# Block 2's mixers: gates by ScalarE's own Silu, a 31-tap convolution over 1024 tokens with its sums in SBUF, and mixer C queued behind it

## The chip, the cores and the metric

The kernel runs on one core of one Trainium2 chip. Its engines work side by side, each on its own list of instructions in a fixed order: PE (TensorE, the matmuls), DVE (VectorE), ACT (ScalarE), POOL (GpSimd) and SP (SyncE, which here issues most of the DMAs). Semaphores tie the lists together: an instruction waits until those it reads from have ended, and all that stands behind it on its engine waits with it. The metric is the device time of one launch in microseconds (us), lower is better. Accumulators of matmuls lie in PSUM, everything else that the engines compute on in SBUF.

## The reference

Two transformer-like blocks over 1024 tokens of width 1024; the change touches only the second, `mix` of the reference. Its input `h` (normalised and modulated) is projected into eleven slots of 512 channels, which feed four mixers; what they give is gated, joined and projected back:

```python
def mix(h, lp, h0, pool_fn):
    proj = jnp.einsum('btd,de->bte', h, lp['w_in'])
    (va, za, bb, bc, bv, zb, ca, cg, zc, dv, zd) = jnp.split(proj, N_IN_SLOTS, axis=-1)
    ya, h_final = rglru(va, lp, h0)
    yb = bb * depthwise_conv(bc * bv, lp['b_conv'], B_CONV // 2, B_CONV // 2)
    u = ca * jax.nn.sigmoid(cg)
    u = depthwise_conv(u, lp['c_conv'], C_CONV // 2, C_CONV // 2)     # C_CONV = 31 taps
    u = layer_norm(u, lp['c_ln_g'], lp['c_ln_b'])
    yc = jnp.einsum('btc,ce->bte', jax.nn.silu(u), lp['c_pw']) + lp['c_pw_b']
    p = pool_fn(dv)
    ...
    cat = jnp.concatenate([ya * jax.nn.silu(za), yb * jax.nn.silu(zb),
                           yc * jax.nn.silu(zc), yd * jax.nn.silu(zd)], axis=-1)
    return jnp.einsum('bte,ed->btd', cat, lp['w_out']), h_final
```

Here silu(z) = z * sigmoid(z), and the depthwise convolution with 31 taps adds, for each channel, 31 shifted copies of its 1024 tokens, each times its own weight.

## The kernel before

Channels lie on the 128 partitions, tokens along the free axis, and the 1024 tokens are two halves of 512 (`HS`). Every large product is made of three matmuls of 128x128 by 128x512: both operands are split into a high part (rounded to fp32r by ACT, a CAST, "hi") and the rest (by DVE, "lo"), and hi·hi, hi·lo and lo·hi are added up in PSUM (lines 411 to 413). A 128x1024 block of weights comes by DMA on SP's queue into a raw tile `wr` and is split into `wh` (ACT, line 367) and `wl` (DVE, line 368); there are three of each, so a raw tile is loaded again only when the `wl` that reads it is done.

`mixers_in` (line 2030 on) computes Block 2's projections with `p2`, one 128-channel chunk of a slot at a time, 8 products a half, on PE from the high/low tiles `kk` of the input. Gates and values that are needed later go to DRAM through `keep` (tile `pk`). The mixers are generators that yield a cost after each step and stand in lists; `tick(n, q)` runs steps of a list until their costs reach n. `fill(a, b)` between two projections runs 4 units (`FA`) of the background list `bg` (mixers A and D) and 3 units (`FB`) of the list `convs`. So the order in which the program is written down mixes projections with mixer steps.

- Mixer A (`mixer_a`, `rg_gates`, `rg_decay`, `rg_scan`; tiles `va`, `xc`, `xh`) is a gated recurrence, mixer D (`mixer_d`; `ph`, `pl`) a box mean followed by a small product.
- Mixer B is written in line at the end of `mixers_in` (`m`, `y`, and the gate `sg` at lines 2092 to 2094).
- Mixer C: `c_in` makes `u` = 2·ca·sigmoid(cg) (tiles `cu`). `conv31` (line 2011) adds the 31 taps of one 128-channel chunk up in two PSUM tiles `pp`, one for a half, so each tap is two instructions of DVE; ACT copies the sums back into `cu` (2028). When all four are done, at c = 3 of the last loop, the rest of `convs` is run to its end (2074) and `mixer_c` is put in `bg` (2076). `mixer_c`, for one half after the other: adds the four chunks (`la`), means by a matmul with ones (`mu`), squares (`acc`, ones matmul at 465), `rs` by Ln and Exp (447, 448), then for each chunk `ln`, `lt` and `sc` (2127 to 2134), and for each output chunk its weights `wch`/`wcl`, 12 matmuls, `yc` (2144) and the product with its gate (`cz`, `cat_out`).

A silu is made of the Tanh function on ACT and DVE instructions, with factors 0.5 folded in: z·sigmoid(z) = 0.5·(tanh(z/2)+1)·z. ACT holds one set of function tables at a time; where the next function lies in another set, an ACT_TABLE_LOAD stands before it.

`tail` projects the joined outputs back: `dense(pair, half, ticks)` loads eight tiles `cr` of `cat` from DRAM, splits them into `cx` (ACT 469, DVE 470), and runs 8 output chunks of 24 matmuls, with 5 units of `bg` after each in the first two calls. What is left of `bg` is flushed before `dense(1, 0)`.

The instructions are not issued in written order. The kernel records them and a list scheduler inside it sets the order on each engine by estimated costs and by data and tile dependences; that order is fixed when the program is built.

Of the kernel before, what the change touches and what calls it, by code (L numbers as in the profile page):

```python
# [11 lines left out]
AF = mybir.ActivationFunctionType  # L12
ALU = mybir.AluOpType
# [5 lines left out]
T = 1024  # L19
HALF = 512  # L20
# [278 lines left out]
HS = [slice(0, HALF), slice(HALF, T)]  # L299


class Build:
# [1680 lines left out]
    def keep(self, slot, c, silu=False):  # L1983

        nc = self.nc
        d = self.dp.tile([P, T], F32, name=f"p2{slot}{c}")

        def epi(ps, sl, hf):
            t = self.F2("pk")
            if silu:  # L1990
                nc.scalar.activation(t, ps, AF.Tanh, scale=0.5)
                nc.vector.scalar_tensor_tensor(t, t, 1.0, ps, op0=ALU.add, op1=ALU.mult)
            else:
                nc.scalar.copy(t, ps)
            self.dma(d[:, sl], t, q="scalar")
        self.p2(slot, c, epi)
        return d

    def cat_out(self, i, c, y, z, hf):

        t = self.T2("cz")
        self.dma(t, z[:, HS[hf]])
        self.nc.vector.scalar_tensor_tensor(t, y, 0.5, t, op0=ALU.mult, op1=ALU.mult)
        self.cat_store(i, c, t, hf)

    def cat_store(self, i, c, t, hf):
# [1 line left out]
        self.dma(d, t, q="scalar")  # L2008
        self.cat[i, c, hf] = d

    def conv31(self, c, u):

        nc = self.nc
        w = lambda j: self.CW[:, 31 * c + j:31 * c + j + 1]
        acc = [self.pp(), self.pp()]
        for hf, sl in enumerate(HS):
            nc.vector.tensor_scalar(acc[hf], u[:, sl], w(15), None, op0=ALU.mult)
        for j in range(31):
            s = j - 15
            if s == 0:  # L2020
                continue
            for hf in range(2):
                a, b = max(HALF * hf, -s), min(HALF * hf + HALF, T - s)
                o = acc[hf][:, a - HALF * hf:b - HALF * hf]
                nc.vector.scalar_tensor_tensor(o, u[:, a + s:b + s], w(j), o, op0=ALU.mult, op1=ALU.add)  # L2025
            yield 1.3
        for hf, sl in enumerate(HS):
            nc.scalar.copy(u[:, sl], acc[hf])

    def mixers_in(self):  # L2030

        self.wide = False
        nc = self.nc
        self.za, self.zd, self.zc = {}, {}, {}
        o = VOFF["c_conv"]
        self.CW = self.V[:, o:o + 124]
        nc.gpsimd.tensor_scalar(self.CW, self.V[:, o:o + 124], 0.5, None, op0=ALU.mult)
        cus = [None] * 4
        m, y = self.S("bm"), self.S("by")
        convs = []  # L2040

        def fill(a, b):
            self.tick(a)
            self.tick(b, convs)

        def c_in(c, halves, ticks):
            if cus[c] is None:
                cus[c] = self.S("cu")
            u = cus[c]
            self.p2(7, c, lambda ps, sl, hf: nc.scalar.activation(u[:, sl], ps, AF.Tanh, scale=0.5), ticks, halves)  # L2050
            self.p2(6, c, lambda ps, sl, hf: nc.vector.scalar_tensor_tensor(u[:, sl], u[:, sl], 1.0, ps, op0=ALU.add, op1=ALU.mult),
                    ticks, halves)
        for c in range(4):
            c_in(c, (0,), N3)
        self.flush()
        for c in range(4):
            c_in(c, (1,), 0)
            convs.append(self.conv31(c, cus[c]))
            fill(0, 6)
        for c in (3, 2, 1, 0):  # L2060
            v, u = self.keep(0, c), self.keep(9, c)
            self.behind(self.mixer_a(c, v))
            self.behind(self.mixer_d(c, u))
            fill(FA, FB)
            fill(FA, FB)
            self.za[c] = self.keep(1, c, True)
            fill(FA, FB)
            self.zd[c] = self.keep(10, c, True)
            fill(FA, FB)
        for c in range(4):  # L2070
            self.zc[c] = self.keep(8, c, True)
            fill(FA, FB)
        for c in range(4):
            if c == 3:
                while convs:
                    self.tick(1, convs)
                self.behind(self.mixer_c(cus))
            self.p2(3, c, lambda ps, sl, hf: nc.scalar.copy(m[:, sl], ps))
            fill(FA, FB)
            self.p2(4, c, lambda ps, sl, hf: nc.vector.tensor_mul(m[:, sl], m[:, sl], ps))  # L2080
            w = lambda tap: self.vec("b_conv", 3 * c + tap)
            nc.scalar.mul(y, m, w(1))
            nc.vector.scalar_tensor_tensor(y[:, 1:], m[:, :T - 1], w(0), y[:, 1:], op0=ALU.mult, op1=ALU.add)
            nc.vector.scalar_tensor_tensor(y[:, :T - 1], m[:, 1:], w(2), y[:, :T - 1], op0=ALU.mult, op1=ALU.add)
            fill(FA, FB)
            self.p2(2, c, lambda ps, sl, hf: nc.vector.tensor_mul(y[:, sl], y[:, sl], ps))
            self.dump(f"y_b{c}", y)
            fill(FA, FB)

            def epi(ps, sl, hf):  # L2090
                t = self.F2("sg")
                nc.scalar.activation(t, ps, AF.Tanh, scale=0.5)
                nc.vector.scalar_tensor_tensor(t, t, 1.0, ps, op0=ALU.add, op1=ALU.mult)
                nc.vector.scalar_tensor_tensor(t, y[:, sl], 0.5, t, op0=ALU.mult, op1=ALU.mult)
                self.cat_store(1, c, t, hf)
            self.p2(5, c, epi)
            fill(FA, FB)

    def mixer_c(self, us):

# [215 lines left out]
```

## Time and profile before

| | us |
|---|---|
| median of 3 runs | 2543.75 (2543.48 to 2548.24) |
| profiled execution | 2544.9 |
| its span, first to last instruction | 2543.1 |
| PE busy | 2476.3 (97%) |
| DVE, ACT busy | 1727.1 (68%), 1188.1 (47%) |
| Block 2's mixers and tail, by the timeline | about 1810 to 2330, and 2330 to 2543 |

Times in rows of the profile are in us from the start of the span unless marked ns. `mm<-cx,wh` reads "a matmul that writes the PSUM tile mm from cx and wh"; `[1.34 <-ACT cx L469]` says that the engine stood idle for 1.34 us before this instruction and that the write of `cx` by ACT at line 469 ended the wait. Matmuls overlap: each is shown longer than the distance between their starts. ACT's instructions overlap a little too.

### The profile page before, as it was taken

What the parts mean: (1) busy time and instruction counts of PE and PEld (TensorE: products, weight loads), DVE (VectorE), ACT (ScalarE), POOL (GpSimd) and SP (SyncE); (2) the same over time, 40 slices, a digit from 0 to 9 for tenths busy, and PEclk for the clock granted to TensorE, in tenths of its full rate; (3) what the DMA queues carried; (4) which work ended last, traced back from release to release, by engine and by line L of the source; (5) the groups of instructions that cost most, each with busy time, mean ns of one, the idle gap of its engine ahead of it and who ended that gap; (6) DMA issues with size and microseconds to landing.
All of it is one profiled execution on the core that took longest, in us unless ns stands there. A gap on an engine that the chain in (4) does not pass through costs nothing. (4 is left out here: it accounts for less than half of the span.)

```text
span 2543.1 us, 33781 instructions
## 1 busy us (share of the span) xinstructions
PE 2476.3 (97%) x12732; PEld 2004.7 (79%) x12732; DVE 1727.1 (68%) x2647; ACT 1188.1 (47%) x1843; POOL 182.1 (7%) x238
## 2 busy tenths in 40 slices
PE   8999999999999999999999999999999999999997
PEld 7887888776777678877788888887888888887886
DVE  7536765664755436758867864457798999996744
ACT  5425554622514357147644543435536355445623
POOL 0000000120111111630000000000000000000000
PEclk9999999999999799999999999999999999999998
DMA  6365443683775567868676565556533333325732
GB/s 218 106 210 160 140 134 105 186 250 104 230 205 157 164 210 233 287 193 278 235 257 221 180 204 180 187 187 224 183 119 113 133 134 97 113 91 192 247 100 100
DMA packets 180085, 449.23 MB, mean 177 GB/s; under 512 B 32145, under 2 KB 42257, under 8 KB 179921
## 3 DMA queue, kind: packets, MB, share of 16 engines
q1 hardware_dynamic: 141504, 342.44, 40.5%
q0 software_dynamic: 18576, 64.63, 9.1%
q10 hardware_dynamic: 19840, 40.00, 4.3%
q8 instruction: 100, 1.64, 0.3%
q14 instruction: 65, 0.52, 0.1%
HBM read 321.55 MB, written 125.44 MB: 176 GB/s over the span
## 5 line engine op out<-in xcount | busy, mean ns | idle before, releaser
L367 ACT CAST wh<-wr 128x1024 fp32r<-128x1024 f32 x243 | 255.0, 1049 | 496.3 <-PE mm L412 246.5
L368 DVE TENSOR_TENSOR wl<-wr,wh 128x1024 fp32r<-128x1024 f32 x243 | 299.5, 1233 | 222.4 <-ACT wh L367 215.9
L411 PE MATMUL mm<-h,wh 128*128 128x512 f32 x760 | 308.1, 406 | 4.0 <-ACT h L469 2.1
L412 PE MATMUL mm<-h,wh 128*128 128x512 f32 x760 | 305.9, 403 | 0.8 <-DVE h L470 0.8
L413 PE MATMUL mm<-h,wl 128*128 128x512 f32 x760 | 304.7, 401 | 0.0
L411 PE MATMUL mm<-kk,wh 128*128 128x512 f32 x704 | 275.2, 391 | 0.0
L412 PE MATMUL mm<-kk,wh 128*128 128x512 f32 x704 | 274.5, 390 | 0.5 <-DVE kk L1811 0.5
L413 PE MATMUL mm<-kk,wl 128*128 128x512 f32 x704 | 274.0, 389 | 0.0
L411 PEld LDWEIGHTS mm<-h,wh 128*128 128x128 f32 x760 | 144.9, 191 | 37.2 <-ACT h L469 3.3
L412 PEld LDWEIGHTS mm<-h,wh 128*128 128x128 f32 x760 | 144.9, 191 | 33.7 <-issue 3.6
L413 PEld LDWEIGHTS mm<-h,wl 128*128 128x128 f32 x760 | 144.6, 190 | 32.7 <-issue 2.9
L2025 DVE SCALAR_TENSOR_TENSOR pp<-cu,vec,pp 128x512 f32<-128x512 f32 (+9 forms) x240 | 166.3, 746 | 0.1
L412 PEld LDWEIGHTS mm<-kk,wh 128*128 128x128 f32 x704 | 132.1, 188 | 29.1 <-issue 1.0
L411 PEld LDWEIGHTS mm<-kk,wh 128*128 128x128 f32 x704 | 132.1, 188 | 28.3 <-issue 0.7
L413 PEld LDWEIGHTS mm<-kk,wl 128*128 128x128 f32 x704 | 132.1, 188 | 27.7 <-issue 0.2
L1539 PE MATMUL pp<-h,wh 128*128 128x512 f32 x320 | 126.2, 397 | 3.8 <-ACT x L1606 2.2
L1540 PE MATMUL pp<-h,wh 128*128 128x512 f32 x320 | 124.8, 390 | 1.4 <-DVE h L470 1.4
L1541 PE MATMUL pp<-h,wl 128*128 128x512 f32 x320 | 123.6, 389 | 0.0
L1748 PE MATMUL pp<-bl,wh 128*128 128x512 f32 x304 | 120.1, 395 | 2.4 <-DVE bl L470 1.7
L1749 PE MATMUL pp<-bh,wl 128*128 128x512 f32 x304 | 119.1, 392 | 0.0
L1747 PE MATMUL pp<-bh,wh 128*128 128x512 f32 x304 | 116.5, 391 | 1.6 <-ACT bh L474 1.6
L411 PE MATMUL mm<-cx,wh 128*128 128x512 f32 x256 | 99.8, 391 | 1.3 <-ACT cx L469 1.3
(562 smaller groups left out, 5434.8 us busy)
## 6 DMA issues: line engine op xcount, KB each, us to landing
wr<-in_wi_dram SPq DMA_DIRECT2D x77, 512.0 KB, 3.4
ws<-in_wm_dram POOLq DMA_DIRECT2D x48, 512.0 KB, 5.8
wr<-in_wo_dram SPq DMA_DIRECT2D x48, 512.0 KB, 3.7
wr<-in_wg_dram SPq DMA_DIRECT2D x32, 512.0 KB, 4.4
gt<-gt POOLq DMA_DIRECT2D x64, 256.0 KB, 4.6
g<-gt SPq DMA_DIRECT2D x64, 256.0 KB, 4.9
wm<-in_wm_dram SPq DMA_DIRECT2D x32, 512.0 KB, 5.0
br<-buB SPq DMA_DIRECT2D x32, 512.0 KB
```

Source lines behind the costliest of these rows:

```text
L367: self.nc.scalar.copy(hi, raw)
L368: self.nc.vector.tensor_sub(lo, raw, hi.bitcast(F32))
L411: M(ps, lhsT=ah, rhs=bh, start=start and i == 0, stop=False)
L412: M(ps, lhsT=ah, rhs=bl, start=False, stop=False)
L413: M(ps, lhsT=al, rhs=bh, start=False, stop=stop and i == last)
L1539: M(ps, lhsT=ah, rhs=bh, start=start and i == 0, stop=False, skip_group_check=True)
L1540: M(ps, lhsT=ah, rhs=bl, start=False, stop=False, skip_group_check=True)
L1541: M(ps, lhsT=al, rhs=bh, start=False, stop=i == last, skip_group_check=True)
L1747: M(banks[p], lhsT=wh[:, o], rhs=bh[:, r], start=first, stop=False, skip_group_check=True)
L1748: M(banks[p], lhsT=wh[:, o], rhs=bl[:, r], start=False, stop=False, skip_group_check=True)
L1749: M(banks[p], lhsT=wl[:, o], rhs=bh[:, r], start=False, stop=jj == 7 and e == 1, skip_group_check=True)
L2025: nc.vector.scalar_tensor_tensor(o, u[:, a + s:b + s], w(j), o, op0=ALU.mult, op1=ALU.add)
```

## The change

Three things are edited. Every silu of a gate from a projection (`keep` with `silu`, mixer B's `sg`) becomes one ACT instruction with the function Silu, and the multiplication with the gate becomes a plain `tensor_mul` on DVE; the silu inside `mixer_c` stays with Tanh. `conv31` works over all 1024 tokens in one SBUF tile `co` of the pool S, one DVE instruction a tap, whose first tap (j = 15) is an ACT multiplication; the copy back goes, and a tap yields 1.2 in place of 1.3. `mixer_c` is appended to `convs`, behind the last convolution, when the list is built; the run of `convs` to its end at c = 3 goes, and what is left of `convs` after the last projection is added to `bg`.

```diff
         def epi(ps, sl, hf):
             t = self.F2("pk")
             if silu:
-                nc.scalar.activation(t, ps, AF.Tanh, scale=0.5)
-                nc.vector.scalar_tensor_tensor(t, t, 1.0, ps, op0=ALU.add, op1=ALU.mult)
+                nc.scalar.activation(t, ps, AF.Silu)
...
-        self.nc.vector.scalar_tensor_tensor(t, y, 0.5, t, op0=ALU.mult, op1=ALU.mult)
+        self.nc.vector.tensor_mul(t, y, t)
         self.cat_store(i, c, t, hf)
...
-    def conv31(self, c, u):
+    def conv31(self, c, us):
         nc = self.nc
+        u = us[c]
         w = lambda j: self.CW[:, 31 * c + j:31 * c + j + 1]
-        acc = [self.pp(), self.pp()]
-        for hf, sl in enumerate(HS):
-            nc.vector.tensor_scalar(acc[hf], u[:, sl], w(15), None, op0=ALU.mult)
+        o = self.S("co")
+        nc.scalar.mul(o, u, w(15))
         for j in range(31):
             s = j - 15
             if s == 0:
                 continue
-            for hf in range(2):
-                a, b = max(HALF * hf, -s), min(HALF * hf + HALF, T - s)
-                o = acc[hf][:, a - HALF * hf:b - HALF * hf]
-                nc.vector.scalar_tensor_tensor(o, u[:, a + s:b + s], w(j), o, op0=ALU.mult, op1=ALU.add)
-            yield 1.3
-        for hf, sl in enumerate(HS):
-            nc.scalar.copy(u[:, sl], acc[hf])
+            a, b = max(0, -s), min(T, T - s)
+            nc.vector.scalar_tensor_tensor(o[:, a:b], u[:, a + s:b + s], w(j), o[:, a:b], op0=ALU.mult, op1=ALU.add)
+            yield 1.2
+        us[c] = o
...
             c_in(c, (1,), 0)
-            convs.append(self.conv31(c, cus[c]))
+            convs.append(self.conv31(c, cus))
+            if c == 3:
+                convs.append(self.mixer_c(cus))
             fill(0, 6)
...
         for c in range(4):
-            if c == 3:
-                while convs:
-                    self.tick(1, convs)
-                self.behind(self.mixer_c(cus))
             self.p2(3, c, lambda ps, sl, hf: nc.scalar.copy(m[:, sl], ps))
...
                 t = self.F2("sg")
-                nc.scalar.activation(t, ps, AF.Tanh, scale=0.5)
-                nc.vector.scalar_tensor_tensor(t, t, 1.0, ps, op0=ALU.add, op1=ALU.mult)
-                nc.vector.scalar_tensor_tensor(t, y[:, sl], 0.5, t, op0=ALU.mult, op1=ALU.mult)
+                nc.scalar.activation(t, ps, AF.Silu)
+                nc.vector.tensor_mul(t, y[:, sl], t)
                 self.cat_store(1, c, t, hf)
             self.p2(5, c, epi)
             fill(FA, FB)
+        self.bg += convs
```

The diff does not show what the scheduler makes of it. Each list below is one engine's order, first to last; a name carries the tile's number, and `<-` stands between what is written and what is read.

ACT, before, around the end of the projections: `sg_3665` is the last gate of mixer B (its PSUM tile is filled by the last projection), `yc_3670` an output of mixer C's first half, and `cx_3692` the first tile that the tail's matmuls read.

```order
L367 CAST wch_3667_19974<-wcr_3666_19973 128x512
L367 CAST wh_3724_20173<-wr_3723_20171 128x1024
L2092 ACTIVATE sg_3665_19967<-mm_3664_19942 128x512
L2144 ACTIVATE yc_3670_19992<-pp_3669_19979,vec_90 128x512
L469 CAST cx_3692_20065<-cr_3691_20063 128x512
L325 DMA cat131_19971<-sg_3665_19967 128x512
L469 CAST cx_3694_20070<-cr_3693_20068 128x512
```

ACT now, at the same place; `sg_3647` is that last gate, `lt` and `ln` belong to the layer norm of mixer C's first half, and `cx_3653` is the tail's first tile.

```order
L2123 ACTIVATE lt_3679_19853<-ln_3678_19851,sm_3622_19589 128x512
L2086 ACTIVATE sg_3647_19742<-mm_3646_19717 128x512
L2124 ACTIVATE ln_3678_19851<-ln_3678_19851,vec_90 128x512
L367 CAST wh_3693_19913<-wr_3692_19911 128x1024
L325 DMA cat131_19745<-sg_3647_19742 128x512
L469 CAST cx_3653_19765<-cr_3652_19763 128x512
L367 CAST wch_3681_19860<-wcr_3680_19859 128x512
L469 CAST cx_3655_19770<-cr_3654_19768 128x512
```

The layer norm of mixer C's first half stood far ahead of the tail's first tile, with some of that half's outputs between; now its last steps stand right before that tile, behind the last gate, and the outputs come later. On PE the ones matmul of that half's squares stood 121 rows ahead of the tail's first matmul (rows 10044 and 10165) and now stands 49 rows ahead of it (10092 and 10141); each of those 49 rows but the first is a projection on `kk`.

PE, before, in the second half of mixer C inside the tail, rows 10331 to 10336: `pp_3740` is the first product that reads the normalised `sc`, `mm_3772` a chunk of the tail's first half.

```order
L413 MATMUL mm_3772_20433<-cx_3704_20095,wl_3767_20398 128x512
L411 MATMUL mm_3772_20433<-cx_3706_20100,wh_3766_20397 128x512
L411 MATMUL pp_3740_20265<-sc_3684_20051,wch_3738_20260 128x512
L412 MATMUL pp_3740_20265<-sc_3684_20051,wch_3738_20260 128x512
L412 MATMUL mm_3772_20433<-cx_3706_20100,wh_3766_20397 128x512
L413 MATMUL mm_3772_20433<-cx_3706_20100,wl_3767_20398 128x512
```

PE now, the same place, rows 10382 to 10387: `pp_3740` is again that product, and `cx_3778` is the first tile of the tail's second half, `dense(0, 1)`.

```order
L413 MATMUL mm_3776_20329<-cx_3667_19800,wl_3771_20294 128x512
L411 MATMUL pp_3740_20129<-sc_3708_19995,wch_3738_20124 128x512
L412 MATMUL pp_3740_20129<-sc_3708_19995,wch_3738_20124 128x512
L411 MATMUL mm_3800_20409<-cx_3778_20357,wh_3774_20325 128x512
L411 MATMUL mm_3804_20441<-cx_3778_20357,wh_3798_20405 128x512
L413 MATMUL pp_3740_20129<-sc_3708_19995,wcl_3739_20125 128x512
```

The ones matmul of this half's squares stood at row 10270 and stands at 10341, so that from it to the first product on `sc` there were 63 rows and are 42. The first matmul on a tile of `dense(0, 1)` stood at row 10407, 137 rows behind the ones matmul, and stands at 10385, 44 behind it. PE's list up to row 8146 is the same in both programs, and each has 11010 rows; DVE's list goes from 2606 to 2445 rows, ACT's from 1895 to 1900. Of ACT_TABLE_LOADs from this stage on there were 28, and there are 37.

## Rows read from the trace of the kernel before

**Rows 1.** Page, busy time of each engine, its share of the span, x instructions.

```profile
PE 2476.3 (97%) x12732; PEld 2004.7 (79%) x12732; DVE 1727.1 (68%) x2647; ACT 1188.1 (47%) x1843; POOL 182.1 (7%) x238
```

**Rows 2.** Windows: sum, PE, PEld, DVE, ACT, POOL busy (records), clock, DMA share, GB/s.

```profile
1950.00:1975.00 25.00, 25.00 (x112) 20.71 (x111) 24.92 (x29) 14.96 (x20) 2.55 (x3) 1.00 0.27 95
...
2325.00:2350.00 25.00, 23.66 (x104) 19.14 (x103) 16.04 (x24) 10.73 (x18) 0.00 (x0) 1.00 0.83 297
```

**Rows 3.** Waits, waiter <- releaser: sum, count, longest; PE from 1800, SP 2200 to 2420.

```profile
PE pp L1394 <- DVE acc L1389: 2.3, 1, 2.3
...
PE pp L411 <- ACT ph L469: 1.5, 2, 1.1
...
PE mm L411 <- ACT cx L469: 1.3, 1, 1.3
...
SPq L372 <- DVE wl L368: 151.6, 23, 16.5
```

**Rows 4.** DVE groups, 1800 to the end: busy us, mean ns | idle before, releaser.

```profile
L2025 DVE SCALAR_TENSOR_TENSOR pp<-cu,vec,pp 128x512 f32<-128x512 f32 x120 | 89.4, 750 | 0.0
...
L2017 DVE TENSOR_SCALAR pp<-cu,vec 128x512 f32<-128x512 f32 x8 | 5.7, 747 | 0.0
...
L1850 DVE SCALAR_TENSOR_TENSOR xc<-va,vec,xc 128x1023 f32<-128x1023 f32 x4 | 5.1, 1285 | 5.2 <-ACT xc L1845 5.2
...
L1992 DVE SCALAR_TENSOR_TENSOR pk<-pk,mm 128x512 f32<-128x512 f32 x24 | 16.4, 684 | 0.6 <-ACT pk L1991 0.4
...
L2093 DVE SCALAR_TENSOR_TENSOR sg<-sg,mm 128x512 f32<-128x512 f32 x8 | 5.4, 681 | 4.8 <-ACT sg L2092 4.8
...
L470 DVE TENSOR_TENSOR cx<-cr,cx 128x512 fp32r<-128x512 f32 x32 | 20.6, 686 | 5.5 <-ACT cx L469 5.5
...
L368 DVE TENSOR_TENSOR wl<-wr,wh 128x1024 fp32r<-128x1024 f32 x84 | 102.6, 1221 | 17.6 <-ACT wh L367 16.0
```

**Rows 5.** ACT groups, same stretch and columns.

```profile
L2028 ACT COPY cu<-pp 128x512 f32<-128x512 f32 x8 | 4.6, 587 | 3.8 <-DVE pp L2025 3.3 <-ACT pk L1994 0.4
...
L1845 ACT ACTIVATE xc<-va,vec 128x1024 f32<-128x1024 f32 x8 | 9.2, 1151 | 2.8 <-DMA va<-p 2.8
...
L1991 ACT ACT_TABLE_LOAD x3 | 3.8, 1283 | 0.5 <-ACT pk L1994 0.4
```

**Rows 6.** Timeline of ACT, end of Block 2's mixers: start, length, [idle before <- releaser].

```profile
2312.86 0.71 ACT L2129 ACTIVATE lt<-ln,sm 128x512 f32<-128x512 f32 x1
...
2313.47 0.62 ACT L2133 ACTIVATE sc<-ln 128x512 fp32r<-128x512 f32 x1
...
2313.99 0.71 ACT L2130 ACTIVATE ln<-ln,vec 128x512 f32<-128x512 f32 x1
...
2329.01 1.05 ACT L367 CAST wh<-wr 128x1024 fp32r<-128x1024 f32 x1 [1.54 <-PE mm L412]
...
2329.97 0.59 ACT L2092 ACTIVATE sg<-mm 128x512 f32<-128x512 f32 x1
...
2332.61 0.61 ACT L469 CAST cx<-cr 128x512 fp32r<-128x512 f32 x1
```

**Rows 7.** Timeline of PE, the first matmul of the tail.

```profile
2333.27 0.97 PE L411 MATMUL mm<-cx,wh 128*128 128x512 f32 x3 [1.34 <-ACT cx L469]
```

**Rows 8.** Timeline of PE and ACT, second half of mixer C, inside the tail.

```profile
2357.92 1.03 PE L465 MATMUL pp<-acc,ones 128*128 128x512 f32 x2
...
2359.69 1.28 ACT L448 ACT_TABLE_LOAD   x1
...
2360.99 0.63 ACT L448 ACTIVATE rs<-rs 128x512 f32<-128x512 f32 x1
...
2371.40 0.62 ACT L367 CAST wch<-wcr 128x512 fp32r<-128x512 f32 x1 [0.25 <-DMA wcr<-in_wcp_dram]
...
2372.88 0.39 PE L411 MATMUL pp<-sc,wch 128*128 128x512 f32 x1
```

**Rows 9.** Tile cat: from a transfer's issue to its landing.

```profile
DMA to landing us min/median/max: 2.0/5.1/8.1
```

## The prediction

> **What bounds the kernel now.** The page's busy times come first: PE is busy for 97% of the span, DVE for 68%, ACT for 47% [rows 1]. So time can only come from what PE waits for, and the next view is the windows over Block 2's mixers and the tail. In the mixers DVE is as full as PE: from 1950 to 1975 it works for 24.92 of 25.00 us, ACT for 14.96, and PE for all 25.00 [rows 2]. Its window holds 112 records, about two of them cut at an edge, so PE starts a matmul every 25.00/110 = 0.227 us. From 2325 on PE has a hole (23.66 of 25.00) while DVE has fallen to 16.04. The third view, PE's waits from 1800 to the end, says how much a full DVE costs: nearly nothing. The largest are 2.3 us for the last `acc` at the very end, 1.5 us in two waits for mixer D's `ph`, and 1.3 us for `cx`, the tail's first tile [rows 3]; what is left adds up to about 1 us. An engine that is full beside a PE that does not wait is off the path. The last view is the order of instructions on ACT, DVE and PE at the two places where mixer C meets the tail, with lengths from the timelines [rows 6 to 8].
>
> **The change part by part.**
>
> Convolution. Before: 240 instructions of DVE on PSUM; the 120 full ones take 750 ns each, and the 120 that are a little narrower no more, so up to 179 us; with the 8 first taps (5.7 us) 185 us [rows 4]. Now: 120 on SBUF over 1009 to 1023 tokens. The trace has that shape in mixer A at 1285 ns, so 120 x 1.285 = 154 us at most, and DVE saves about 31 us. On ACT 8 copies go (4.6 us) and 4 multiplications of 1.15 us come (4.6 us): nothing. If a tap in SBUF cost as much as two halves (1.50 us), nothing is saved, and since PE does not wait for DVE there, nothing is lost either.
>
> Silu. On DVE 24 instructions of `keep` go (16.4 us) and 8 of mixer B (5.4 us) [rows 4]; the remaining products change form, not number. DVE in all: about -53 us, of which PE can collect only its own waits. I let the wait for `ph` go, which DVE's queue feeds: -1.3 of 1.5 us (bounds 0 and -1.5). Of the hole at the end nothing goes, since the last `acc` is far behind the change.
>
> Tables. Silu lies in another set than Sigmoid, and the program has 9 more ACT_TABLE_LOADs from this stage on. One takes 1283 ns [rows 5], so ACT gets 9 x 1.28 = 11.5 us more. In the mixers ACT works 14.96 of 25 us, and a projection's half gives it 24 x 0.227 = 5.4 us before the next result, so I take 0 there (bounds 0 and +11.5); if that cover is gone, each load delays the copy that frees a PSUM tile. In rows 8 the ACTIVATE behind a load starts 0.02 us after its end (2359.69 + 1.28, then 2360.99), so the load is the whole price seen. The Trainium skill, page "ScalarE: Activation LUTs", section "What ACT_TABLE_LOAD costs", puts a switch of sets at about 2.66 us, the load and a drain of about 1.38 us, and the section "Table sets: the hidden batching unit" has kernels group work by set. By the page the nine would take 24 us of ACT and my forecast would be 1.4 us higher, for the one load at the first place below; this trace shows the load's length and not the drain.
>
> First place: the tail's first matmul. `mixer_c` now runs behind the list of convolutions and not when the last convolution is forced, and so comes later against PE. From the ones matmul of its first half's squares to the tail's first matmul there were 121 rows of PE; there are 49. I set that ones matmul's start to 0 and replay the three lists. PE needs 0.63 us more for it than for others (rows 8: 14.96 us to the 63rd row behind it, 63 x 0.227 = 14.3), so PE arrives at 0.63 + 49 x 0.227 = 11.75. On ACT `rs` ends at 3.70 (2360.99 + 0.63 - 2357.92, with the same load in it), DVE gives the first `ln` at 4.5, and then ACT's list holds: `lt`, a load for Silu (1.28), `sg`, and `ln`, `lt` and `sc` of the chunks, at starts 0.61, 0.52 and 0.62 us apart [rows 6], with DVE's products in between (about 0.7 each), until the last `lt` ends at 12.25. Then come the last gate `sg_3647`, which needs PE's last projection, `ln_3678`, `wh_3693` (0.96 from start to start, rows 6) and `cx_3653` (0.61): `cx` is ready at about 15.05, a wait of 3.3. Its low part is on DVE behind `wl_3694` (1.22 us) and takes 0.69 [rows 4]: PE's second matmul waits 1.1 more, its fifth, behind `wcl`, about 0.65. And on SP the load of `wr_3749` stands ahead of the last three `cr`; it waits for `wl_3694` to free a raw tile, as SP did for 151.6 us in 23 waits of that kind [rows 3]. These `cr` then land 2.0 to 8.1 us after issue, 5.1 in the middle [rows 9]: PE gets there at about 20.2, the tiles at 18.6 to 24, so I add 1.0 (0 to 4). In all 3.3 + 1.75 + 1.0 = 6.05, less the 1.34 that PE waited there before [rows 7]: **+4.7**. Lower bound: only what stands on ACT behind PE's last projection, sg 0.5 + ln 0.62 + wh 0.96 + cx 0.61 = 2.7, so +1.4. Upper: no overlap on ACT (cx a further 0.95 later) and a late `cr`, +8.
>
> Second place: the second half of mixer C. From its ones matmul to the first product on `sc` there were 63 rows; there are 42. PE arrives at 0.63 + 42 x 0.227 = 10.2. Before, the weights `wch` were cast by 2372.02, 14.1 after the ones matmul, and PE came at 14.96 without a wait [rows 8]. Now a `wh` of 1 us less stands in that chain, and by the same replay `wch` ends at about 12.9: a wait of 2.7. Two rows later PE needs `cx_3778` of the tail's second half, which ACT casts behind `sc_3711`: 0.9 more; two rows later `wcl`, behind a `wl` and a `sc` on DVE: 0.8 more. **+4.4** (bounds +2, when the chain gains 0.7 and DVE is ahead, and +7.4, without overlap and with late `cr`). Before, `dense(0, 1)` began 137 rows behind the ones matmul and none of this was near.
>
> The sum: 4.7 + 4.4 - 1.3 = +7.8 on the profiled execution's 2544.9, that is 2552.7. That execution was 1.15 above the median of the runs shown, so the forecast on their scale is **2551.5 us**. About 0.2%, 5.1 us, is what a measurement of this kernel can tell from no change: slower begins at 2548.8, faster at 2538.7.
>
> **The rivals.**
>
> A, the forecast: both places make PE wait, about 2551.5. For it: the order on each engine is fixed, the chains behind the ones matmuls hold only work that the trace has lengths for, and PE brings too few rows to cover them. Against it: the order in which cr and weights arrive is not fixed.
>
> B, not slower: DVE's relief pays for the places. They cost their lower bounds, +1.4 and +2, because a DVE without a backlog answers ACT at once; and the waits before them go (`ph` 1.5 and about 1 for the others): 2543.75 + 3.4 - 2.5, about 2544.7. It decides if the two places together wait under 8 us (the 1.34 of before included), with DVE idle before each step of `ln`. For it: DVE falls by 53 us just ahead of the first place. Against it: these chains are mostly ACT's own instructions.
>
> C, the table loads reach PE as well. In the mixers a load before a `keep` or `sg` delays a PSUM tile that PE wants; half of the 11.5 us on top of the 7.8: 2543.75 + 7.8 + 5.8, about 2557, and 1.3 more if the wait for `ph` stays too. For it: loads stand right before copies that free PSUM tiles. Against it: of the 28 loads before none shows as a releaser in PE's waits, which name tiles that were late by 1.5 us in sum at most.
>
> D, faster: DVE was the hidden bound. Waits of 3.9 us vanish, and the tail's tiles are ready in time because all of mixer C runs earlier: 2544.9 - 3.9 - 1.15, about 2540. Against it: the order on PE itself puts mixer C's steps nearer to the tail, so C cannot run earlier than PE's own list allows.
>
> **How the numbers follow.** A 0.56, B 0.25, C 0.13, D 0.06. Slower by over 0.2% is A less a small part near its lower end, and C: 0.67. Within 0.2%: B and that part, 0.27. Faster: 0.06. The range goes from 2544.5, just under B (both lower bounds, and every other wait gone), which leaves out D and the part of B below it, to 2558, near both upper bounds (2543.75 + 15.4 - 1.3 = 2557.9) and the middle of C. A alone would be 2547 to 2557.
>
> **What would show it.** In the profile after: DVE's convolution as 120 instructions of about 1.28 us, and windows between 1950 and 2275 with DVE well below 25 us while PE stays at 25.00; no `ph` wait. PE's waits should hold 3 to 4 us for ACT's `cx` at the tail's first matmul, with `cx` of DVE or `cr` just behind, and some 4 us for `wch`, `cx` and `wcl` 42 to 46 rows after the second ones matmul. Right before the first, ACT's timeline should show the last gate, `ln`, `wh` and `cx` without a gap. The prediction is wrong if PE passes both places with under 3 us of wait (B or D), or if its waits before 2325 grow (C).

## The result and the profile after

The changed kernel is slower: 2566.03 us median of 6 launches (2553.77 to 2570.57) against 2543.61 for the kernel before on the same chip, a ratio of 1.0077 (95% interval 1.0048 to 1.0106). Measured again in 12 launches it was 1.0059 (1.0031 to 1.0086). The sign of the forecast was right, its size was not: +7.8 us were forecast, some 15 to 22 came, and 2566 lies above the range.

Launches of one program spread over 20 us here, so what moves by a few us is read from the traces. One stretch serves as a measure: from the first projection matmul of Block 2 (the first that reads `kk`) to the end. It starts at 1811.72 in the trace before and at 1803.69 in the trace after; what differs ahead of it is no work of the change (in the window from 840 to 860 the granted clock was 0.51 in the first and 0.83 in the second). The stretch took 2543.1 - 1811.72 = 731.4 us before and 2552.0 - 1803.69 = 748.3 after: +16.9. Second traces of the two kernels gave 730.5 and 749.6.

The page after, line of busy times, against [rows 1]: DVE fell by 39 us (53 were forecast) and ACT rose by 13, PE's own work is the same.

```profile
PE 2476.8 (97%) x12732; PEld 2004.9 (79%) x12732; DVE 1687.8 (66%) x2487; ACT 1201.0 (47%) x1848; POOL 182.1 (7%) x238
```

The window that [rows 2] shows, after the change: DVE was to be well below 25 us there and is not. It has room in other windows (11.71 of 25 us from 1925 on, 16.50 from 2125 on).

```profile
1950.00:1975.00 25.00, 25.00 (x112) 20.70 (x111) 25.00 (x26) 8.09 (x13) 2.55 (x3) 1.00 0.32 116
```

PE's waits from 1800 to the end of the trace after, the view of [rows 3]:

```profile
PE mm L411 <- ACT cx L469: 4.5, 2, 4.1
PE pp L411 <- ACT ph L469: 4.2, 2, 2.2
PE pp L411 <- ACT wch L367: 2.3, 1, 2.3
PE pp L1394 <- DVE acc L1389: 2.3, 1, 2.3
PE pp L412 <- DVE pl L470: 0.9, 2, 0.8
PE pp L411 <- ACT xh L469: 0.9, 1, 0.9
```

`cx` went from 1.3 to 4.5 us, `wch` came with 2.3, as forecast; `ph` did not go but grew from 1.5 to 4.2, and `pl` and `xh` are new. The waits sum to some 10 us more than before. The rest is TensorE's clock. Windows around the tail's first matmul (columns as in [rows 2]):

```profile
2326.00:2328.00 2.00, 0.00 (x0) 0.00 (x0) 1.76 (x3) 2.00 (x4) 0.00 (x0) 1.00 1.00 263
2328.00:2330.00 2.00, 1.41 (x3) 0.81 (x4) 2.00 (x4) 1.65 (x3) 0.00 (x0) 0.50 1.00 360
...
2332.00:2334.00 2.00, 2.00 (x6) 1.52 (x6) 0.34 (x1) 0.00 (x0) 0.00 (x0) 0.50 0.83 268
...
2334.00:2335.00 1.00, 1.00 (x5) 0.77 (x4) 0.27 (x1) 0.62 (x1) 0.00 (x0) 0.58 0.80 252
...
2336.00:2338.00 2.00, 2.00 (x10) 1.27 (x9) 1.39 (x2) 0.96 (x2) 0.00 (x0) 1.00 1.01 362
```

After 4 us without work PE resumes at half its clock (0.50, the 1.2 GHz level; six records in 2 us where the full clock has ten) and stays there for nearly 7 us, until shortly before 2335. The timelines of ACT and PE at that place, which answer to [rows 6] and [rows 7]:

```profile
2311.98 1.04 ACT L367 CAST wh<-wr 128x1024 fp32r<-128x1024 f32 x1 [4.00 <-PE mm L412]
...
2316.34 0.63 ACT L448 ACTIVATE rs<-rs 128x512 f32<-128x512 f32 x1
...
2325.35 0.57 ACT L2086 ACTIVATE sg<-mm 128x512 f32<-128x512 f32 x1
2325.83 0.71 ACT L2124 ACTIVATE ln<-ln,vec 128x512 f32<-128x512 f32 x1
2326.44 1.03 ACT L367 CAST wh<-wr 128x1024 fp32r<-128x1024 f32 x1
...
2327.38 0.61 ACT L469 CAST cx<-cr 128x512 fp32r<-128x512 f32 x1
```

```profile
2328.04 0.79 PE L411 MATMUL mm<-cx,wh 128*128 128x512 f32 x1 [4.15 <-ACT cx L469]
2329.38 0.79 PE L412 MATMUL mm<-cx,wh 128*128 128x512 f32 x1 [0.55 <-DVE cx L470]
...
2330.40 0.63 PE L411 MATMUL mm<-cx,wh 128*128 128x512 f32 x1
2330.83 0.63 PE L412 MATMUL mm<-cx,wh 128*128 128x512 f32 x1
```

The last gate, `ln`, `wh` and `cx` stand on ACT without a gap, as forecast. (The first two rows are the start of that chain and are taken up again where the two places are weighed against the prediction.) From one matmul to the next it is now 0.43 us (2330.40 to 2330.83) in place of 0.227. The second place, PE's timeline, against [rows 8]:

```profile
2378.19 1.12 PE L465 MATMUL pp<-acc,ones 128*128 128x512 f32 x2
...
2390.94 0.50 PE L411 MATMUL pp<-sc,wch 128*128 128x512 f32 x1 [2.30 <-ACT wch L367]
...
2393.03 0.80 PE L413 MATMUL pp<-sc,wcl 128*128 128x512 f32 x1 [0.31 <-DVE wcl L368]
```

And mixer D's product near 2181, PE's timeline: a wait of 2.25, and half clock behind it (0.43 from start to start).

```profile
2181.16 0.75 PE L411 MATMUL pp<-ph,wdh 128*128 128x512 f32 x1 [2.25 <-ACT ph L469]
2181.70 0.63 PE L411 MATMUL mm<-kk,wh 128*128 128x512 f32 x1
2182.13 0.63 PE L412 MATMUL mm<-kk,wh 128*128 128x512 f32 x1
```

To weigh these I add up by how much the distance between PE's starts exceeds 0.227 us a matmul, place by place. First place: 1.5 before, 8.0 after. Second place: 0.6 and 5.4. Mixers A and D (`ph`, `pl`, `xh`, `xl`, with the half clock behind them): 2.3 and 8.8. Together +17.8, which is the stretch's 16.9 and a little that went elsewhere. Some 6 us of the 17.8 are half clock. So the mixers, ahead of the tail, gave +6.5 and the two places +11.3.

### The profile page after: what moved, and what is told of

It is laid out like the page before. It is cut to its first block, busy times and chain, and to the rows that moved or that the text cites. A ratio compares the mean times of both kernels' runs of the same rounds, so it can differ in the third digit from the quotient of the medians.

```text
span 2552.0 us, 33598 instructions
## 1 busy us (share of the span) xinstructions
PE 2476.8 (97%) x12732; PEld 2004.9 (79%) x12732; DVE 1687.8 (66%) x2487; ACT 1201.0 (47%) x1848; POOL 182.1 (7%) x238
## 4 chain that ended last, share of the span: by engine, by line
PE 71%; DVE 13%; DMA 6%; ACT 5%; issue 3%; SPq 1%; POOL 0%; ACTq 0%; DVEq 0%; POOLq 0%
PE mm L412 11%; PE mm L411 11%; PE mm L413 11%; PE pp L1539 3%; PE pp L1541 3%; PE pp L1540 3%; PE pp L411 3%; PE pp L412 3%; PE pp L413 3%; PE pp L1748 2%; PE pp L1749 2%; PE pp L1747 2%; DVE co L2022 2%; PE pp L634 2%; DVE wl L368 1%
## 5 line engine op out<-in xcount | busy, mean ns | idle before, releaser
L2022 DVE SCALAR_TENSOR_TENSOR co<-cu,vec,co 128x1009 f32<-128x1009 f32 (+14 forms) x120 | 152.6, 1271 | 1.1
```

Source lines behind the costliest of these rows:

```text
L2022: nc.vector.scalar_tensor_tensor(o[:, a:b], u[:, a + s:b + s], w(j), o[:, a:b], op0=ALU.mult, op1=ALU.add)
```

## The experiments

All of them go by the stretch; the ratio to the kernel before, of 7 to 12 launches, stands beside it.

| kernel | stretch, us | ratio (95% interval) |
|---|---|---|
| before, two traces | 731.4, 730.5 | 1.0033 (1.0005 to 1.0061) |
| after, two traces | 748.3, 749.6 | 1.0059 (1.0031 to 1.0086) |
| Silu alone | 737.5 | 1.0010 (0.9984 to 1.0035) |
| Silu's places with a copy | 734.2 | 1.0014 (0.9987 to 1.0041) |
| convolution alone | 732.5 | 1.0002 (0.9972 to 1.0032) |
| convolution alone, taps in halves | 736.0 | 1.0018 (0.9986 to 1.0050) |
| convolution alone, two DMAs on other queues | 737.6 | 1.0011 (0.9984 to 1.0038) |
| queueing alone | 745.6 | 1.0035 (1.0010 to 1.0061) |
| all but the queueing | 739.5 | 1.0019 (0.9993 to 1.0045) |
| after, TensorE kept busy | 752.5 | 1.0063 (1.0033 to 1.0093) |
| after, `du` on GpSimd's queue | 745.8 | 1.0054 (1.0028 to 1.0079) |
| after, mixer C further ahead | 745.2 | 1.0061 (1.0030 to 1.0092) |

The first row's ratio is that of the unchanged kernel to itself: at this size a ratio within about 0.3% of 1 says nothing, interval or not (the prediction had taken 0.2%). The stretch is steadier, but only two kernels were traced twice, and the queueing alone, below, has nearly 4 us of its stretch from a transfer that landed late. So a single trace that differs by less than some 4 us is a hint and no proof.

**The kernel before, again.** 

> The kernel before, unchanged, traced a second time: how far Block 2's stretch moves by itself. Theory 1 (the stretch is steady, the spread of 20 us between launches comes from the clock ahead of it): 731.4 within 2 us. Theory 2 (the landing of transfers such as du moves it): 734 or more, with a longer wait for ph, as in the kernel where only the queueing was changed (2.5 us there).

 It took 730.5, with the same waits to 0.05 us, but for an `xh` of 0.3 that came and a `wch` of 0.4 that went: theory 1. **The changed kernel, again.** 

> The changed kernel, unchanged, traced a second time. Theory 1 (waits follow from the order and lengths of the instructions): the same waits within 0.5 us, cx 4.1, wch 2.3, ph 2.2 and 1.95, stretch 748.3 within 2 us; the stretch of half clock may move. Theory 2 (they were that run's chance): some of them under 1 us. In launches, 17 us (0.66%) above before.

 It took 749.6; `cx` again waited 4.15 and `wch` 2.29, `ph` 1.60 and 1.95, and another `wch` 0.85. The first waits at the two places repeat to 0.01 us; the one behind `cx`, for its low part, was 0.84 in place of 0.55; the first `ph` moved by 0.65 us, the second not at all, and the half clock fell behind the second `ph` this time and not behind the first.

**Silu alone.**

```diff
-                nc.scalar.activation(t, ps, AF.Tanh, scale=0.5)
-                nc.vector.scalar_tensor_tensor(t, t, 1.0, ps, op0=ALU.add, op1=ALU.mult)
+                nc.scalar.activation(t, ps, AF.Silu)
```

> Only the gates use Silu; convolution and the queueing of mixer C are as before. The stretch from the first projection matmul of Block 2 to the end took 731.4 us before and 748.3 after the whole change. Theory 1 (the added time comes from mixer C's place in the queue and from the longer convolution instructions on VectorE): this kernel's stretch is within 1.5 us of 731.4, waits for ph stay at 1.5 us or less, no clock drop. Theory 2 (the added table loads hold ScalarE up, and the casts behind it are late): 5 us or more longer, with new waits of PE for ph, xh or cx.

 Theory 1 fell: 737.5. Its waits of PE, the two that grew most:

```profile
PE pp L411 <- ACT ph L469: 2.9, 2, 1.4
PE pp L411 <- ACT wch L367: 2.5, 2, 1.5
```

Behind the first `ph` wait, of 1.41 us, the clock fell here too, which cost some 1.7 us:

```profile
2174.00:2176.00 2.00, 2.00 (x5) 1.60 (x6) 2.00 (x3) 0.72 (x2) 0.00 (x0) 0.56 0.00 1
```

**A copy in Silu's places**, in both of them; the kernel is otherwise that with Silu alone.

```diff
-                nc.scalar.activation(t, ps, AF.Silu)
+                nc.scalar.copy(t, ps)
```

> As the kernel with Silu alone, but with a plain copy in place of Silu (the gate's function is left out, so what is computed differs): VectorE's instructions are the same, and of the 100 table loads 81 are left. Silu alone took 737.5, 6.1 us more than before. Theory 1 (table loads, and what they delay in ScalarE's order, make most of that): within 2 us of 731.4, waits for wch gone. Theory 2 (VectorE's saved instructions let the scheduler put PE's ph and xh matmuls earlier than their data are ready): still 736 or more.

 It took 734.2, between the two theories: 3.3 us of Silu's cost go with the table loads, about 3 stay. The half clock is in the 3.3, and so is what the scheduler does otherwise without the loads, since the orders of the two kernels part in Block 2's mixers; the loads by themselves were not isolated. The same two rows, here:

```profile
PE pp L411 <- ACT ph L469: 1.5, 2, 0.9
PE pp L411 <- ACT wch L367: 1.5, 3, 0.6
```

How a table load can get from ACT, which is half idle, to PE can be followed. ACT's loads ahead of mixer A's Sigmoid (line 1860), first before (and the same with the copy), then with Silu alone:

```profile
L1860 ACT ACT_TABLE_LOAD x4 | 5.1, 1283 | 0.1
```

```profile
L1860 ACT ACT_TABLE_LOAD x9 | 11.5, 1283 | 0.2
```

A Silu that falls among the Sigmoids makes ACT load twice: the loads ahead of the gates' function (line 1991) went from 3 to 8. Mixer A goes from ACT to DVE and back, and DVE's order puts its scans and products ahead of a split of weights, `wl`. That split frees the raw tile for which SP's queue waits, and behind the load that waits stands the one of mixer D's input `du`. SP's timeline with Silu alone, then with the copy:

```profile
2127.01 26.27 SPq L372 DMA_DIRECT2D wr<-in_wi_dram  x2
2153.33 0.43 SPq L325 DMA_DIRECT2D du<-p  x1
```

```profile
2137.84 22.26 SPq L372 DMA_DIRECT2D wr<-in_wi_dram  x2
2160.15 0.42 SPq L325 DMA_DIRECT2D du<-p  x1
```

Counted from each trace's first `kk` matmul (1799.55 and 1810.46), `du` is issued at 353.8 with Silu and at 349.7 with the copy; it was 349.5 before and 355.1 after. So 4 to 5.6 us were lost ahead of mixer D, in a stretch in which DVE has room (13.01 of 25 us from 2125 on, with Silu alone). Of the 4.1 us between Silu and the copy, 1.5 are there when mixer A's Sigmoid starts (328.0 and 326.5), behind one load more of 1.28. The other 2.6 come behind it, and a part of them is order: with Silu two products `cz` (1.2 us) stand ahead of that `wl`, with the copy behind it. DVE's timeline with Silu alone, then with the copy:

```profile
2150.51 1.28 DVE L2002 TENSOR_TENSOR cz<-xc,cz 128x512 f32<-128x512 f32 x2
2151.71 1.22 DVE L368 TENSOR_TENSOR wl<-wr,wh 128x1024 fp32r<-128x1024 f32 x1
```

```profile
2158.53 1.22 DVE L368 TENSOR_TENSOR wl<-wr,wh 128x1024 fp32r<-128x1024 f32 x1
2159.66 1.29 DVE L2002 TENSOR_TENSOR cz<-xc,cz 128x512 f32<-128x512 f32 x2
```

From `du`'s first copy on ACT some 14 to 17 us of steps that pass between ACT and DVE follow until `ph` is cast. In the changed kernel the whole delay arrives there (376.8 in place of 371.3), with Silu alone only 1.3 of 4.3 us (372.6). So this chain explains a part of Silu's cost and not all.

**Convolution alone.**

```diff
+        o = self.S("co")
+        nc.scalar.mul(o, u, w(15))
...
+            a, b = max(0, -s), min(T, T - s)
+            nc.vector.scalar_tensor_tensor(o[:, a:b], u[:, a + s:b + s], w(j), o[:, a:b], op0=ALU.mult, op1=ALU.add)
```

> Only the convolution is changed (one 1024-token instruction a tap, sums in SBUF); gates and queueing as before. Theory 1: waits for ph, pl and xh grow from 1.5 to about 6 us, one of them long enough that the clock falls behind it; stretch about 6 us longer than 731.4, places at the tail unchanged. Theory 2: VectorE has 31 us less work and PE's waits for ph go: 1 us shorter or equal.

 It took 732.5: +1.5 against the mean of the two traces before, with `ph` at 2.9 and `pl` at 0.9. Neither theory: the waits grew, by half of what theory 1 wanted, and the stretch by little more than it moves from trace to trace (1.0 and 1.3). **The same with a tap in two halves.**

```diff
-            a, b = max(0, -s), min(T, T - s)
+            for hf in range(2):
+                a, b = max(HALF * hf, -s), min(HALF * hf + HALF, T - s)
```

> The convolution alone is changed, with sums in SBUF, but each tap in two instructions of 512 tokens as before. The kernel with one instruction a tap took 732.5, with waits for ph and pl of 3.8 us in all. Theory 1 (a tap twice as long, standing in the middle of mixer D's chain, delays ph): waits for ph and pl back to 1.5 us, stretch 731. Theory 2 (the waits come from the scheduler's other order, with two PSUM tiles more to spare): 732.5 or more, ph and pl as there.

 It took 736.0, with waits of 2.2 for `ph`, 1.9 for `xl` and 1.4 for `pl`. So short taps do not take the waits away, and theory 1 fell. That the order which the scheduler makes of a convolution in SBUF delays mixer D is what is left (theory 2); what in that order does it stays open, and 3.5 us between two single traces do not settle more. **The same with `du` loaded and the gated outputs stored by GpSimd's queue.**

```diff
-        self.dma(d, t, q="scalar")
+        self.dma(d, t, q="gpsimd")
...
-        self.dma(u, d)
+        self.dma(u, d, q="gpsimd")
```

> The convolution alone is changed (one instruction a tap), gates and queueing as before; mixer D's input du is loaded, and the gated outputs are stored, by GpSimd's queue in place of SyncE's and ScalarE's, so that ScalarE does not stand behind a store that waits for VectorE. Theory 1 (what is left of PE's waits in Block 2 comes from such queues): ph under 1 us, stretch 728 to 731. Theory 2 (stores on GpSimd's queue land later and delay the tail's cr): cx wait over 2 us, 733 or more.

 It took 737.6, with a `ph` wait of 2.4 and half clock behind it; `cx` stayed at 1.3. Theory 1 fell. But the `du` ahead of that wait was issued no earlier than with the convolution alone (352.1 in place of 351.1 behind the first `kk` matmul), so the run does not tell what an earlier `du` would do.

**Queueing alone.**

```diff
+            if c == 3:
+                convs.append(self.mixer_c(cus))
...
-                while convs:
-                    self.tick(1, convs)
-                self.behind(self.mixer_c(cus))
...
+        self.bg += convs
```

> Only the queueing of mixer C is changed; convolution and gates as before. Theory 1: the two places at the tail appear as after the whole change, a wait for cx of about 4 us and one for wch of about 2 us, each followed by some 5 us at half clock: stretch about 10 to 12 us longer than 731.4; the waits for ph as before, 1.5 us. Theory 2: the queueing alone costs nothing, under 2 us.

 It took 745.6. `cx` waited 3.5 at the first place and `wch` 2.3 at the second, each with half clock behind it: theory 1. A part is not the queueing's. Ahead of the first `ph` wait the order on PE, ACT, DVE and SP's queue is that of before, and `du` was issued at the same time (349.5), but it landed later. ACT's timeline, before and here:

```profile
2166.91 0.62 ACT L2177 COPY pa<-du 128x512 f32<-128x512 f32 x1 [2.36 <-DMA du<-p]
```

```profile
2174.75 0.62 ACT L2176 COPY pa<-du 128x512 f32<-128x512 f32 x1 [4.48 <-DMA du<-p]
```

These 2.1 us arrive whole at PE: the first `ph` waited 2.52 in place of 0.41, with half clock behind, some 3.7 us in all. With nothing else changed, this is the plainest sign that the first `ph` wait follows `du`.

**All but the queueing.** The change with the forced run of the list and `behind` put back.

> The whole change but for the queueing of mixer C, which is forced and appended as before. Theory 1: the sum of the two single parts, about 5 to 6 us longer than 731.4, with ph, pl and xh waits and without the wait for cx of 4 us. Theory 2: about as long as the whole change, 748.

 It took 739.5, 8.5 more than before (mean of two), which is near Silu's 6.5 and the convolution's 1.5 put together. The first place has 1.7 for `cx`. The queueing is then worth 748.9 - 739.5 = 9.4 us, with the half clock in it. Some 2 of these are again `ph`: the orders are the same up to the tail, but in the kernel without the queueing the clock did not fall behind the `ph` waits (1.85 and 1.96).

**TensorE kept busy at the first place**, with three extra matmuls behind the last gate.

```diff
+                if c == 3 and hf == 1:
+                    ps2 = self.pp()
+                    for _ in range(3):
+                        nc.tensor.matmul(ps2, lhsT=self.ones, rhs=t, start=True, stop=True)
```

> The changed kernel, with three extra fp32 matmuls (ones by the last gate's tile, 128x512, into a PSUM tile that nobody reads) on TensorE between the last projection and the tail's first matmul; ScalarE's order is the same. They run once the last gate is done, so that some 2.6 us of the wait for cx of 4.1 us are work. Theory 1 (the clock falls because TensorE stood idle for those 4 us, and that costs some 3 us behind the wait): the first matmul of the tail comes at the same time as before, but no stretch at half clock follows, and the stretch is about 3 us shorter than the changed kernel's 748.3. Theory 2 (the half clock has another cause, the transfers that run at the same time, or chance): the half clock stays and the stretch is 748 or longer.

 PE's timeline (the first row holds the three extra ones) and a window of its clock:

```profile
2335.57 2.84 PE L2092 MATMUL pp<-sg,ones 128*128 128x512 f32 x6 [2.81 <-DVE sg L2087]
2337.85 0.79 PE L411 MATMUL mm<-cx,wh 128*128 128x512 f32 x1
```

```profile
2338.00:2340.00 2.00, 2.00 (x9) 1.46 (x9) 2.00 (x5) 1.29 (x3) 0.00 (x0) 1.00 1.01 335
```

The first matmul of the tail came later by 0.9 us (5.47 us behind the last projection's start, 4.53 after), and yet the full clock stayed: some thirty matmuls on, this kernel was 1.7 us ahead of the changed one, counted from the last projection (PE's order differs there, with products on `sc` sooner). PE stood idle for 2.81 us even here, longer than at other waits behind which the clock fell, and it did not fall. Theory 1 holds at this place, as far as one trace tells: the four traces with that wait and without the extra matmuls (the changed kernel twice, the queueing alone, `du` on the other queue) all have the fall. The stretch as a whole did not shrink, since the scheduler also moved the second place:

```profile
2390.18 0.70 PE L465 MATMUL pp<-acc,ones 128*128 128x512 f32 x1
...
2404.14 0.79 PE L411 MATMUL pp<-sc,wch 128*128 128x512 f32 x1 [7.82 <-ACT wch L367]
```

There the ones matmul stands 23 rows ahead of the product. With 63 rows PE did not wait, with 42 it waited 2.30, with 23 it waited 7.82. Of the last 5.5 us, 19 rows of 0.227 are 4.3; the rest is the chain, which ended 1.2 us later (13.96 behind the ones matmul in place of 12.75). So the wait is set mostly by the rows between them.

**`du` on GpSimd's queue, in the changed kernel.** The second of the two edits above.

> The changed kernel, with mixer D's input du loaded by GpSimd's DMA queue in place of SyncE's, where it stands behind loads of weights that wait for a free raw tile. Theory 1 (PE's waits for ph are set by the late start of mixer D's chain, the landing of du): the wait for ph of 2.2 us near 2178 goes, and the clock drop behind it too, 3 to 5 us less than 748.3. Theory 2 (the waits come from the longer convolution instructions that stand on VectorE inside the chain): the wait stays over 1.5 us.

 It took 745.8; the first `ph` wait was 1.30 in place of 2.25, without half clock, the second stayed at 1.95. `du` was issued some 40 us earlier, but ACT took it up only 3.5 us sooner (2168.3 in place of 2171.8, both on the time scale of the trace before). ACT's timeline shows why:

```profile
2173.56 1.05 ACT L367 CAST wh<-wr 128x1024 fp32r<-128x1024 f32 x1 [8.33 <-DVE cz L2002]
2174.93 1.15 ACT L2076 ACTIVATE by<-bm,vec 128x1024 f32<-128x1024 f32 x1 [0.31 <-DVE bm L2074]
2175.99 0.60 ACT L2171 COPY pa<-du 128x512 f32<-128x512 f32 x1
```

The copy of `du` stands behind a store of mixer A's `cz`, for which ACT waits 8.33 us (8.12 at that place before), so it is the same late mixer A that holds mixer D, now through ACT's list. Theory 1 in part; the chain has more than one way to be late, and the second `ph` wait is left without a cause.

**Mixer C further ahead.**

```diff
-NL, N1, N2, N4, N3, FA, FB = 6.0, 3.0, 3.0, 2.4, 2.5, 4.0, 3.0
+NL, N1, N2, N4, N3, FA, FB = 6.0, 3.0, 3.0, 2.4, 2.5, 4.0, 4.0
```

> The changed kernel with 4 in place of 3 units of the convolution list between two projections, so that mixer C runs further ahead: its first ones matmul of squares stands some 467 rows of TensorE ahead of the tail's first matmul in place of 49, and all of mixer C is done before the tail. Theory 1 (the place of mixer C, not the queueing as such, costs the two waits at the tail): no wait for wch in the tail, cx within 1.5 us, no clock drop there: 735 to 740. Theory 2 (what is gained there is lost in the mixers, where VectorE is full earlier): 745 or more.

 It took 745.2, near theory 2. The second place is gone, but a wait of 4.5 us for mixer B's `bm` came in the mixers, and `cx` still waited 3.8. ACT's timeline at the first place shows another reason for it:

```profile
2347.01 0.59 ACT L2086 ACTIVATE sg<-mm 128x512 f32<-128x512 f32 x1
2348.99 0.33 ACTq L325 DMA_DIRECT2D cat<-sg  x1
2349.36 2.70 ACT L469 CAST cx<-cr 128x512 fp32r<-128x512 f32 x5 [1.76 <-DVE sg L2087]
```

The store of the last gate stands ahead of `cx` in ACT's list and waits 1.76 us for DVE's product, which stands behind a `wl`. Before, `cx` stood ahead of that store. No version was found that beats the kernel before.

## Why the prediction was wrong, step by step

**What bounds the kernel**: right. PE's work is the same, DVE's 39 us less bought nothing.

**The convolution**: a tap was sized well (120 instructions, 1271 ns in the middle, for a bound of 1285), what it saves was not. The sum added up the lengths of the 240 instructions before, up to 179 us, but neighbours overlap there, and they filled 166.3 us of DVE. So with the first taps DVE saved 19 us and not 31:

```profile
L2025 DVE SCALAR_TENSOR_TENSOR pp<-cu,vec,pp 128x512 f32<-128x512 f32 (+9 forms) x240 | 166.3, 746 | 0.1
```

```profile
L2022 DVE SCALAR_TENSOR_TENSOR co<-cu,vec,co 128x1009 f32<-128x1009 f32 (+14 forms) x120 | 152.6, 1271 | 1.1
```

Nothing of it reached PE. The effect on the path was put at nothing; it was +1.5 by itself, little more than two traces of one kernel differ by.

**The wait for `ph` and the table loads**: these are the steps that failed. "I let the wait for `ph` go, which DVE's queue feeds: -1.3" and "so I take 0 there" for the loads. Measured without the queueing, the two parts that were to give -1.3 gave +8.5. The prediction had named the sign for it: PE's waits before 2325 grew, from some 2 us to 6.6. The `ph` wait does not shrink with DVE's work: DVE had 39 us less to do and it grew from 1.5 to 4.2. It hangs on a chain over ACT, DVE and SP's queue, of which the landing of `du` is one link (2.1 us later, 2.1 us more wait, in the queueing alone) and mixer A, ahead of it, another; one of the added table loads stands in that chain. The cover that I named, 5.4 us of projection for each load, protects what the projection's next result needs; it does not protect a chain that runs over ACT, DVE and SP's queue for tens of us. Rival C had the loads, but with a PSUM tile as the way to PE, which no trace shows, and with 5.8 us where 3.3 were found, order and half clock among them. How much is the loads' own stays open. The other 3 us of Silu stay with a copy in its place, so they are no table loads; that they are an order which the scheduler made otherwise is what is left, and where they arise is not settled beyond the waits for `wch` (1.5 in place of 0.4) and `cx` (1.7 in place of 1.3).

**The two places**: their mechanism and their site were right, the sum nearly so, with terms of the wrong kind, so that it came near is in part luck. First place: 3.3 + 1.75 + 1.0 were forecast for `cx`, low parts and late `cr`; it was 4.15 + 0.55 + 0 in waits, and about 3 in half clock, +6.5 in all against +4.7. PE arrived 11.8 us behind the ones matmul, as computed (11.75); `cx` was ready at 16.0 and not at 15.05. The replay had taken `rs` from [rows 8], done 3.70 behind the ones matmul; here it was done at 5.0, since a cast of `wh` (1.04 us) stood ahead of its table load. The late `cr` came late, but PE at half clock did not have to wait for them. Second place: 2.7 + 0.9 + 0.8; it was 2.30 + 0.31 + 0.31 in waits and some 2 of half clock, +4.8 against +4.4. Against the kernel without the queueing, the two and what they shift come to 9.4, `ph` included, where 9.1 stood in the sum. **The half clock** is the second step that failed: it was nowhere in the prediction and is some 6 us of what came. Both windows of [rows 2] show a clock of 1.00. A sign of it was in that trace all the same: behind the one long wait before, the 2.3 us for the last `acc` [rows 3], the clock fell to 0.50 (windows 2528 to 2532 and 2532 to 2536: 0.77 and 0.50), where next to no matmul was left to pay for it.

**The page on table loads**: the trace after has 1283 ns a load and the next ACTIVATE 0.01 to 0.02 us behind it (2319.83 behind 2318.54 + 1.28), so the drain that the Trainium skill, page "ScalarE: Activation LUTs", section "What ACT_TABLE_LOAD costs", adds does not show here either. This trace differs from the page in that. Its section "Table sets: the hidden batching unit" tells kernels to group by set; that rule spoke against this change, and Silu alone, with its 11 loads more, took 6.5 us longer, of which 3.3 went with the copy.

## What to carry to other kernels

An engine that is half idle on average can still be on the path: ask of each added instruction not whether its engine has room, but which chain it stands in, over all engines and in-order DMA queues, and what that chain's slack is at its end. A step that is moved to another place costs what the rows between it and its reader no longer cover; count these rows in the order before costing anything else. And a new wait of TensorE of some us is to be priced with a stretch of half clock behind it, as a risk: it came behind most of the waits of over 2 us here, and cost 1.5 to 3 us each.

## What the runs showed of the hardware

TensorE's clock fell to 0.50 behind waits of 4.15, 2.30 and 2.25 us in the changed kernel, of 3.52, 2.52 and 2.29 in the queueing alone, and once behind one of 1.41 (Silu alone, at 2174). It stayed at 1.00 behind waits of 1.85 and 1.96 in the kernel without the queueing and behind one of 2.81 where TensorE was kept busy right after it; and the same 1.95 us for `ph` was followed by half clock in one trace of the changed kernel and not in the other. So a wait's length alone does not tell. Each fall cost 1.5 to 3 us, at 0.43 us a matmul in place of 0.227. The spread of launches is found ahead of the stretch: its start lay anywhere from 1797.6 to 1819.4 in the traces, behind work that is the same in all of these kernels, while the length of the stretch repeated within 1.3 us in the two kernels that were traced twice.
